# Residual kept by chunks, merged operands split in two portions, norms on two tiles, and early MLP weights split ahead of time in a transformer block on one core

## The chip, the cores and the metric

The kernel runs on one core of one Trainium2 chip. The metric is device time in microseconds (us) of one execution; the number for a kernel is the median of several timed runs. Engines: PE is the matrix engine, PEld its weight loads, DVE the vector engine, ACT the scalar engine, POOL is GpSimd, and SP is the engine whose queue issues nearly all DMAs of this kernel. Each engine takes its own instructions strictly in the order in which they were built, and waits at an instruction until what it needs is there.

## The reference, cut to what matters

One block on 1024 positions of 1024 channels behind 16 meta tokens (L = 1040), all in float32:

```
h      = rmsnorm(h_res, g_mix_pre)
u, c, b, v, gates = split(h @ w_in)
y_a    = fourier_mix(u) @ w_fourier            # real part of a 2-D DFT
y_b    = (b * dwconv3(c * v)) @ w_conv_out
merged = gates_0 * y_a + gates_1 * y_b
h_res  = h_res + rmsnorm(merged @ w_out, g_mix_post)
h2     = rmsnorm(h_res, g_ffn_pre)
a, v   = split(dwconv3(h2 @ w_up))             # 2 x 2816 columns
h_res  = h_res + rmsnorm((gelu(a) * v) @ w_down, g_ffn_post)
```

## The kernel before, in words

Activations lie transposed: a tile has 128 channels on the partitions and positions along the row, so 1024 channels are 8 tiles (`KT`). Every float32 matmul is made of three products of rounded operands of type fp32r (`mm3`, L163, L165, L167): an operand is *split* into a rounded part `hi`, a copy on ACT (L131, shown as CAST), and the rest `lo`, a subtraction on DVE (L132); the three products are hi·hi, lo·hi and hi·lo. The large products are made in seven pieces out of four quarters (`b11`, `t1`, `t2`, ...), whose sums and splits are kept in long-lived tiles of a pool (`room`, by tags such as `t1h`, `t3l`).

In order of time:

1. **Projection** (until about 310 us). A list of jobs, one pair of weight blocks each. Raw weights come by SP through a ring of three 512 KB buffers (`ring.raw`), are split, and are used from a ring of split pieces. Hooks in the jobs do work for later stages: `transformed(kt)` loads `wu` into a raw buffer (L609), PE multiplies it (L612, tile `wp`), ACT copies the product back into the same buffer, SP stores it (L617); `fold(kt)` loads, scales and folds the input on DVE and stores it.
2. **Fourier stage and merge** (to 424 us). The gated sum goes to DRAM as `merged_d`.
3. **Output projection** (424 to 523 us). Positions are cut into four chunks of 256 or 258 (`CHM`). `project(c)` makes, for each of 8 output tiles f, 8 times 3 matmuls on 258 columns, tile `mo`; the operands `mh`, `ml` are the split merged tiles of that chunk, the weights are resident. After each f, ACT squares `mo` and copies it, scaled, into `hA` (chunks 0, 1) or `hB` (chunks 2, 3). After some f a hook of other work is placed, at the level of priority of the newest matmul (`behind(x)` means: not ahead of x in the built order). The order inside an engine's queue is then fixed by the scheduler that builds the program. The hooks of chunk c are:
   - after f number 1, `norm_a(c-1)`: sum of squares (`ms_m` on PE), the reciprocal root `rr` (one ACT, three DVE instructions, L172 to L175), then per tile `hA = hA*rr`, plus the residual input `xr`, square on ACT, sum `sq_h` on DVE, and a store of the tile to DRAM as `hres_d` (needed again at the very end of the kernel);
   - after number 5, `load_merged(c+1)` (L929): three loads into raw buffers (`mr`), each followed by the splits of its three tiles into `mh` and `ml` (10 buffers each);
   - after number 6, `norm_b(c-1)` (L1003): `ms_h` on PE (L926), the root, then per tile a scaling (L1011) and the split into the MLP's operand `b11h`, `b11l`, `b21h`, `b21l` (chunks 0, 1), or a difference and the split into `t1`, `b22` (chunks 2, 3).
   In chunk 3 the hooks also load and split the first MLP weights (`plain.load`, `first_blocks`).
4. **Early MLP** (523 to 570 us). While the last two chunks are still normalised, PE works through products that need only the first half of the positions: `plain.first(...)` and `early(step, i)` for i from 1 to 5. Their weights go through the raw ring into rooms by `first_blocks`: 512 KB, two ACT casts and two DVE subtractions per block. Results that are kept for later are copied from the accumulator by ACT (`up_u`, L294; `up_1e`, L1104; `up_s`, L1060), and the accumulators are few, so PE waits for those copies.
5. **MLP** (to about 1000 us): 22 pairs of blocks, each followed by convolution, gelu and a product, with pieces stored in DRAM; then the **down projection** and the last norm, which loads `hres_d` again (`load_residual`) and stores the output.

What sets the order around the change: the hooks' places, the `behind` lines, three raw buffers, ten `m` buffers, four buffers of the tag `o` for `xr`, and the single SP queue for all DMAs.

Of the kernel before, what the change touches and what calls it, by code (L numbers as in the profile page):

```python
# [17 lines left out]
P = 128  # L18
# [25 lines left out]
CHM = [(0, 258), (258, 258), (513, 258), (771, 256)]  # L44
HALF = 512
# [45 lines left out]
def block_kernel(ctx, tc, xT, w_u, w_in, w_fa, w_fa2, w_fb, w_fb2, w_co, w_out, w_up, w_dn,  # L91
# [586 lines left out]
    W = 258  # L678
# [147 lines left out]

    def merged_parts(c, kt, src):
        n = src.shape[-1]
        parts = [
            op.tile([P, W], F32R, tag=f"m{i}", name=f"m{i}{c}_{kt}", bufs=10)[:, :n] for i in "hl"  # L830
        ]
        return parts, split(*parts, src)
# [96 lines left out]
    def load_merged(c):  # L929
        c0, n = CHM[c]  # L930
        v = valid(c)
        parts = []
# [7 lines left out]
        merged[c] = parts  # L940
# [32 lines left out]
    def norm_a(c):  # L973
        c0, n = CHM[c]
        v = valid(c)
        ms = next(z[c])
        rr = np_.tile([P, W], F32, tag="rr", name=f"rr{c}", bufs=2)[:, :n]
        got = rsqrt_of(f"r2_{c}", scratch, ms, n, rr)
        sq = squares(f"h{c}", n)
        next(sq)  # L980
        xr = []
        for f in range(0, KT, 2):
            t = eo.tile([P, 2 * W], F32, tag="o", name=f"xr{c}_{f}", bufs=4)
            t = t.rearrange("p (f n) -> p f n", f=2)
            SP.dma_start(t[:, :, :v], xT[:, f : f + 2, TM + c0 : TM + c0 + v])
            xr += [t[:, i, :v] for i in range(2)]
        for f in range(KT):
            h = h_at(c, f)
            scaled = mul(h, h, rr).ins
            add(h[:, :v], h[:, :v], xr[f])  # L990
            sq.send(h)
            SP.dma_start(hres_d[:, f, c0 : c0 + v], h[:, :v])
        z[c] = sq
        return got, scaled
# [8 lines left out]
    def norm_b(c):  # L1003
# [5 lines left out]
        for f in range(KT):  # L1009
            h = h_at(c, f)  # L1010
            V.scalar_tensor_tensor(out=h, in0=h, scalar=col("g_fpre", f), in1=rr, op0=ALU.mult, op1=ALU.mult)  # L1011
# [15 lines left out]
    def sums(c):  # L1027
        j, n = CHM[c][0] - 513, CHM[c][1]
        A, B = second(c)
        for f in range(4):  # L1030
            sub(A(f), B(f + 4), A(f))
            put(hx["t2"], f, A(f), j, n)
# [8 lines left out]

    class Plain:
# [5 lines left out]
        def load(self, row, name):  # L1048
            r = room(name, F32R, f"pw{row}")
            q = [r[:, k * 512 : (k + 1) * 512] for k in range(4)]  # L1050
            self.w[row] = early_pieces(f"{self.up.name}p{row}", srcs(self.up)[row], (q[:2], q[2:]))
# [120 lines left out]
    def first_blocks(*rooms_):  # L1172
        for n in rooms_:
            i = len(ep)
            into = (None, None)
            if n is not None:
                r = room(n, F32R, f"ep{i}")
                q = [r[:, k * 512 : (k + 1) * 512] for k in range(4)]
                into = (q[:2], q[2:])
            ep.append(early_pieces(firsts[i].name, srcs(firsts[i])[0], into))  # L1180
# [10 lines left out]
    project(0, {4: new_banks, 5: lambda: load_merged(1)})  # L1191
# [348 lines left out]
```

## Time and profile before

| what | us |
|---|---|
| median of 3 runs (lowest, highest) | 1206.96 (1206.75, 1207.26) |
| the profiled execution | 1208.31 |
| its span, first to last instruction | 1206.5 |
| PE busy, share of the span | 1177.1, 98% |
| DVE busy | 1000.9, 83% |
| ACT busy | 552.0, 46% |
| POOL busy | 8.4, 1% |

The profiled execution took 1.35 us more than the median, and 1.81 us of it lie outside the span. Times of day in this text ("at 468 us") are microseconds from the start of that span. In a row of instructions, the first number is the start, the second the busy time of the group, then come engine, line, operation, output<-inputs and shape; an idle time in brackets at the end is the wait just before the group and what ended it. Buffer numbers are left out in those names: `mh` may be any of `mh2_0` to `mh2_7`. In a table of stretches, the columns are the stretch, its length, busy us and number of instructions of PE, PEld, DVE, ACT and POOL, then the granted clock of PE as a share of full speed, the busy share of the DMA engines and the GB/s that they moved.

### The profile page before, as it was taken

The numbers are of one execution on the slowest core, as the hardware profiler recorded it, in microseconds if no ns is written. First come the engines' busy times: TensorE is split into PE (matmuls) and PEld (weight loads), VectorE is DVE, ScalarE is ACT, GpSimd is POOL, SyncE is SP. The second block draws the span as 40 slices with busy tenths as digits, with TensorE's granted clock in tenths as the row PEclk, the third lists the DMA queues.
The fourth block names the chain that finished last, engine by engine and source line by source line (L and its number), as shares of the span: only waits on it lengthen the run. The fifth ranks groups of instructions, "written<-read, shape, count | busy, mean of one in ns | idle before, by whom it ended". The sixth has DMA issues, their size and how long they took to land.

```text
span 1206.5 us, 22298 instructions
## 1 busy us (share of the span) xinstructions
PE 1177.1 (98%) x8790; PEld 1134.4 (94%) x8790; DVE 1000.9 (83%) x1756; ACT 552.0 (46%) x1008; POOL 8.4 (1%) x38
## 2 busy tenths in 40 slices
PE   8999999999999999998999999999999999999995
PEld 7999999999999999998999999999999998888884
DVE  8999976756578956989799999989988989856678
ACT  6743333223352345656544544444344444455562
POOL 0000000000020000000000000000000000000000
PEclk9999999999999999999999999999999999999998
DMA  6336655132876756575243334324323498354433
GB/s 250 123 111 217 194 177 176 53 132 90 276 232 223 256 169 106 141 101 153 98 143 106 121 122 149 123 97 131 97 71 96 139 331 315 101 167 126 135 119 140
DMA packets 79408, 184.25 MB, mean 153 GB/s; under 512 B 8146, under 2 KB 25778, under 8 KB 79304
## 3 DMA queue, kind: packets, MB, share of 16 engines
q1 hardware_dynamic: 79160, 182.71, 48.3%
q8 instruction: 69, 1.13, 0.4%
q14 instruction: 35, 0.29, 0.1%
q10 hardware_dynamic: 144, 0.12, 0.0%
HBM read 131.54 MB, written 51.26 MB: 152 GB/s over the span
## 4 chain that ended last, share of the span: by engine, by line
PE 81%; DVE 12%; DMA 4%; ACT 1%; issue 1%; SPq 0%; DVEq 0%; ACTq 0%
PE up_d L167 3%; PE up_c L165 3%; PE up_c L163 3%; PE up_d L163 3%; PE up_d L165 3%; PE up_c L167 3%; PE up_a L163 3%; PE up_a L167 3%; PE up_a L165 3%; PE dna L163 3%; PE dna L165 3%; PE dna L167 3%; PE dnb L165 2%; PE dnb L163 2%; PE dnb L167 2%; PE up_b L167 2%
## 5 line engine op out<-in xcount | busy, mean ns | idle before, releaser
L163 PE MATMUL mo<-mh,wo 128*128 128x258 f32 (+1 forms) x256 | 74.0, 289 | 0.0
L167 PE MATMUL mo<-mh,wo 128*128 128x258 f32 (+1 forms) x256 | 73.0, 285 | 0.0
L165 PE MATMUL mo<-ml,wo 128*128 128x258 f32 (+1 forms) x256 | 72.9, 285 | 0.0
L165 PEld LDWEIGHTS mo<-ml,wo 128*128 128x128 f32 x256 | 49.3, 193 | 0.2
L163 PEld LDWEIGHTS mo<-mh,wo 128*128 128x128 f32 x256 | 49.2, 192 | 0.2
L167 PEld LDWEIGHTS mo<-mh,wo 128*128 128x128 f32 x256 | 49.2, 192 | 0.0
L131 ACT CAST up_1h<-up_1t 128x512 fp32r<-128x512 f32 x11 | 6.8, 621 | 75.0 <-DVE up_1t L148 52.2
L1134 ACT ACTIVATE up_0o<-up_0o 128x512 f32<-128x512 f32 x44 | 27.8, 631 | 23.5 <-DVE up_0o L1132 23.3
L1130 ACT ACTIVATE up_1o<-up_1x,pr 128x512 f32<-128x512 f32 x33 | 26.9, 816 | 23.0 <-DVE up_1x L148 22.5
L167 PE MATMUL up_d<-b22h,up_5l 128*128 128x258 f32 (+1 forms) x168 | 34.2, 284 | 0.0
L165 PE MATMUL up_c<-t3l,up_3h 128*128 128x258 f32 (+1 forms) x168 | 34.1, 285 | 0.0
L167 PE MATMUL up_b<-t2h,up_2l 128*128 128x258 f32 (+1 forms) x168 | 34.0, 283 | 0.0
L163 PE MATMUL up_d<-b22h,up_5h 128*128 128x258 f32 (+1 forms) x168 | 34.0, 283 | 0.0
L165 PE MATMUL up_d<-b22l,up_5h 128*128 128x258 f32 (+1 forms) x168 | 33.9, 283 | 0.0
L165 PE MATMUL up_b<-t2l,up_2h 128*128 128x258 f32 (+1 forms) x168 | 33.9, 283 | 0.0
L163 PE MATMUL up_c<-t3h,up_3h 128*128 128x258 f32 (+1 forms) x168 | 33.8, 282 | 0.0
L163 PE MATMUL up_b<-t2h,up_2h 128*128 128x258 f32 (+1 forms) x168 | 33.8, 282 | 0.0
L163 PE MATMUL up_c<-t4h,up_6h 128*128 128x258 f32 (+1 forms) x168 | 33.8, 282 | 0.0
L163 PE MATMUL up_d<-t1h,up_1h 128*128 128x258 f32 (+1 forms) x168 | 33.7, 282 | 0.0
L167 PE MATMUL up_d<-t1h,up_1l 128*128 128x258 f32 (+1 forms) x168 | 33.7, 282 | 0.0
L165 PE MATMUL up_d<-t1l,up_1h 128*128 128x258 f32 (+1 forms) x168 | 33.6, 281 | 0.0
L167 PE MATMUL up_c<-t3h,up_3l 128*128 128x258 f32 (+1 forms) x168 | 33.6, 281 | 0.0
(1337 smaller groups left out, 4319.3 us busy)
## 6 DMA issues: line engine op xcount, KB each, us to landing
g<-gp_d SPq DMA_DIRECT2D x35, 512.0 KB, 4.2
up_1r<-in_w_up_dram SPq DMA_DIRECT2D x22, 512.0 KB, 3.6
gp_d<-up_0o SPq DMA_DIRECT2D x44, 256.0 KB, 2.0
up_0r<-in_w_up_dram SPq DMA_DIRECT2D x20, 512.0 KB, 4.1
s<-sig_d SPq DMA_DIRECT2D x16, 514.0 KB, 6.1
sig_d<-g_s SPq DMA_DIRECT2D x30, 257.0 KB, 3.4
u<-fold_d SPq DMA_DIRECT2D x8, 777.0 KB, 4.2
fold_d<-fold SPq DMA_DIRECT2D x8, 521.0 KB, 3.5
```

The costliest lines, as they stand in the source:

```text
L131: a = copy(hi, src)
L163: nc.tensor.matmul(o, wh, h, start=first, stop=False, **kw)
L165: nc.tensor.matmul(o, wh, l, start=False, stop=False, **kw)
L167: newest[:] = [nc.tensor.matmul(o, wl, h, start=False, stop=last, **kw).ins]
L1130: S.activation(t, ap[:, 1 : 1 + HALF], AF.Identity, bias=col("cb_ffn", b), scale=w(1))
L1134: S.activation(t, t, AF.Gelu_apprx_tanh)
```

## The change

**Residual by chunks.** The host passes the residual input a second time as `x_res`, laid out as [chunk, partition, tile, 258]; `hres_d` gets the same layout. A load of `xr` still brings two tiles, but as one run of 2064 bytes per partition in place of two of 1032. `norm_a` works on two tiles at once (multiply by `rr`, add `xr`), and stores two tiles with one DMA: four stores per chunk for eight. `load_residual` at the end makes two loads for each one, because a half of the positions spans two chunks.

**Norms on two tiles.** In `norm_b` and `sums` the scalings stay one tile each, but the differences and the splits (cast and subtraction) take two tiles each.

**Merged operands in two portions.** `load_merged(c+1)` moves from hook 5 to hook 0 (to 3 in chunk 0) and only issues the loads. The splits of tiles 0 to 2 (`MORE = 3`) are at hook 5. Those of tiles 3 to 7 are at hook 7, `last_parts`, behind the ACT casts of `b11` that `norm_b` just made. The `m` tiles get 11 buffers. The memset of the padding goes to GpSimd.

**Early MLP weights.** In projection jobs, at six hooks, `ahead(i)` loads one pair of weight blocks through the raw ring, splits it (two casts, two subtractions on 512 columns) and stores the four parts in DRAM (`split_d`) with four DMAs of 256 KB on GpSimd's queue. `plain.load` and `first_blocks` no longer load raw weights and split; they bring both parts, `hi` and `lo`, with two DMAs of 512 KB each on GpSimd's queue (`split_weights`). Only the last block (`first_blocks(None)`) goes on as before.

The number of PE instructions and their order do not change.

```
 def ahead(i):                                       # new, hooks (NE1 + i, 6), i = 0..5
     for n, parts in enumerate(ring.halves(f"ew{i}", w_up[EARLY_ROWS[i]])):
         for m, t in enumerate(parts):
             at = 512 * (2 * n + m)
             nc.gpsimd.dma_start(split_d[i, :, at : at + 512], t.bitcast(F32))

 def split_weights(i, name):                         # new, for plain.load and first_blocks
     r = room(name, F32R, f"ew{i}")[:, : 4 * 512]
...
     for k in range(0, 4, 2):
         at = slice(k * 512, (k + 2) * 512)
         nc.gpsimd.dma_start(r[:, at].bitcast(F32), split_d[i, :, at])

 def norm_a(c):
...
-            SP.dma_start(t[:, :, :v], xT[:, f : f + 2, TM + c0 : TM + c0 + v])
+            SP.dma_start(t, x_res[c, :, f : f + 2])
...
-        for f in range(KT):
-            h = h_at(c, f)
-            scaled = mul(h, h, rr).ins
-            add(h[:, :v], h[:, :v], xr[f])
-            sq.send(h)
-            SP.dma_start(hres_d[:, f, c0 : c0 + v], h[:, :v])
+        for f in range(0, KT, 2):
+            h = h_two(c, f)
+            scaled = mul(h, h, rr[:, None, :].to_broadcast([P, 2, n])).ins
+            add(h, h, xr[f // 2])
+            for i in range(2):
+                sq.send(h_at(c, f + i))
+            SP.dma_start(hres_d[c, :, f : f + 2, :n], h)

 def load_merged(c):
...
-                V.memset(t[:, :, v:], 0.0)
-            parts += [merged_parts(c, kt, t[:, kt - k])[0] for kt in range(k, e)]
+                nc.gpsimd.memset(t[:, :, v:], 0.0)
+            merged_r[c, k] = t
+def split_merged(c, ks):
+    for kt in ks:
+        merged[c].append(merged_parts(c, kt, merged_r[c, kt // 3 * 3][:, kt % 3])[0])
+def last_parts(c):
+    with behind(*cast):                              # cast: the b11 casts of norm_b
+        split_merged(c, range(MORE, KT))
...
-            1: lambda: norm_a(c - 1), 5: lambda: load_merged(c + 1), 6: lambda: (mean_b(c - 1), norm_b(c - 1)),
+            0: lambda: load_merged(c + 1), 1: lambda: norm_a(c - 1), 5: lambda: split_merged(c + 1, range(MORE)),
+            6: lambda: (mean_b(c - 1), norm_b(c - 1)), 7: lambda: last_parts(c + 1),
```

What the change moves is seen in the built order. First DVE at the boundary of chunk 1 and chunk 2, from the second root (`r3_0_t`, `rrb0`) of chunk 0 on. Before (`hA0`, `hA1` are the two halves of the tiles of chunk 0, `ml2_3` is the `lo` of the merged tile 3 of chunk 2):

```order
L173 SCALAR_TENSOR_TENSOR r3_0_t_5778<-r3_0_y_5777 128x258
L132 TENSOR_TENSOR ml2_2_5718<-mr2_0_5707,mh2_2_5717 128x258
L132 TENSOR_TENSOR ml2_3_5724<-mr2_3_5721,mh2_3_5723 128x258
L132 TENSOR_TENSOR ml2_4_5728<-mr2_3_5721,mh2_4_5727 128x258
L132 TENSOR_TENSOR ml2_5_5732<-mr2_3_5721,mh2_5_5731 128x258
L132 TENSOR_TENSOR ml2_6_5738<-mr2_6_5735,mh2_6_5737 128x258
L132 TENSOR_TENSOR ml2_7_5742<-mr2_6_5735,mh2_7_5741 128x258
L174 SCALAR_TENSOR_TENSOR r3_0_t_5778<-ms_h0_5774,r3_0_t_5778 128x258
```

The same place of DVE's queue in the changed kernel:

```order
L176 SCALAR_TENSOR_TENSOR r3_0_t_5831<-r3_0_y_5830 128x258
L177 SCALAR_TENSOR_TENSOR r3_0_t_5831<-ms_h0_5827,r3_0_t_5831 128x258
L178 SCALAR_TENSOR_TENSOR rrb0_5829<-r3_0_t_5831,r3_0_y_5830 128x258
L1040 SCALAR_TENSOR_TENSOR hA0_5245<-hA0_5245,pr_68,rrb0_5829 128x258 x4
L135 TENSOR_TENSOR b11l_5252<-hA0_5245,b11h_5251 128x2x257
L1040 SCALAR_TENSOR_TENSOR hA1_5246<-hA1_5246,pr_68,rrb0_5829 128x258
L135 TENSOR_TENSOR b11l_5252<-hA0_5245,b11h_5251 128x2x257
L1040 SCALAR_TENSOR_TENSOR hA1_5246<-hA1_5246,pr_68,rrb0_5829 128x258 x3
L151 TENSOR_TENSOR sq_m1_0_5580<-sq_m1_0_5580,sq_m1_7_5877 128x258
L135 TENSOR_TENSOR b21l_5254<-hA1_5246,b21h_5253 128x2x257 x2
L135 TENSOR_TENSOR ml2_3_5882<-mr2_3_5585,mh2_3_5881 128x258
L135 TENSOR_TENSOR ml2_4_5886<-mr2_3_5585,mh2_4_5885 128x258
```

Tiles 3 to 7 of the next chunk's merged operand stood behind one instruction of the root and now stand behind the whole of `norm_b(0)`. On PE, the matmul that reads `ml2_3` is the second one of tile 3, the eleventh of chunk 2 (nine matmuls on tiles 0 to 2 come first). At the boundary of chunks 2 and 3 the order has the same form.

SP's queue in the projection, around the second hook of weights that are split ahead (`wu` of `transformed`, `V0r` raw weights of a later job, `sig_d` and `fold_d` stores). Before:

```order
L617 DMA fold_d_58<-wu1_2153 128x512
L395 DMA sig_d_57<-g0_3_s22_2103 128x514
L204 DMA V0r0_2271<-in_w_in_dram 128x1024
L395 DMA sig_d_57<-g0_3_s11_2188 128x514
L204 DMA V0r1_2273<-in_w_in_dram 128x1024
L395 DMA sig_d_57<-g0_3_s12_2219 128x514
L609 DMA wu2_2402<-in_w_u_dram 128x512
```

And in the changed kernel:

```order
L624 DMA fold_d_58<-wu1_2168 128x512
L402 DMA sig_d_57<-g0_3_s22_2118 128x514
L207 DMA ew1r_2286<-in_w_up_dram 128x1024
L402 DMA sig_d_57<-g0_3_s11_2203 128x514
L207 DMA V0r0_2300<-in_w_in_dram 128x1024
L402 DMA sig_d_57<-g0_3_s12_2234 128x514
L207 DMA V0r1_2302<-in_w_in_dram 128x1024
L402 DMA sig_d_57<-g0_3_s21_2278 128x514
L641 DMA fold_d_58<-fold6_3545 128x1042
L616 DMA wu2_2431<-in_w_u_dram 128x512
```

The ring has three raw buffers and goes round: before, `wu2` takes the buffer that `wu1` had; now, with one load more per job, it takes the one that `ew1r` had. On ACT in the early MLP, the changed kernel has these rows (`up4_1e_0h` and `up1_0_0h` are split from the raw loads `up4_1er` and `up1_0r0`; `up1_1_a` is an accumulator of PE):

```order
L297 COPY up1_1_u_6819<-up1_1_a_6794 128x514
L175 ACTIVATE r3_3_y_6977<-ms_h3_6824,eps_t_72 128x256
L134 CAST up4_1e_0h_6988<-up4_1er_6986 128x512
L134 CAST up4_1e_1h_6992<-up4_1er_6986 128x512
L134 CAST up1_0_0h_7055<-up1_0r0_7051 128x512
L1148 COPY up1_1e_6854<-up1_1_a_6794 128x514
```

In the kernel before, the copy `up1_1e` stands ahead of the casts from `up4_1er` and `up1_0r0`, and behind two pairs of casts of `ep3`.

More of the change, by code (lines that the diff above doesn't have):

```diff
@@ L365, in put, with put2 @@
         split(hi[:, kt, c0 : c0 + n], lo[:, kt, c0 : c0 + n], src, eng=eng)
+    def put2(piece, kt, src, c0=0, n=NH):
+        hi, lo = piece
+        return split(hi[:, kt : kt + 2, c0 : c0 + n], lo[:, kt : kt + 2, c0 : c0 + n], src)
     proj_s = ExitStack()
@@ L654, in next_fold, with ahead @@
         folded.append((xs, (hi[:, FW:w], lo[:, FW:w])))
+    EARLY_ROWS = [0, NF // 2, *(NF + n // 2 for n in EARLY[:-1])]
+    def ahead(i):
+        for n, parts in enumerate(ring.halves(f"ew{i}", w_up[EARLY_ROWS[i]])):
+            for m, t in enumerate(parts):
+                at = 512 * (2 * n + m)
+                nc.gpsimd.dma_start(split_d[i, :, at : at + 512], t.bitcast(F32))
     hooks = {(NE1 + kt, 3): lambda kt=kt: transformed(kt) for kt in range(KT)}
+    for i in range(len(EARLY_ROWS)):
+        hooks[NE1 + i, 6] = lambda i=i: ahead(i)
     for kt in range(KT):
@@ L829, in merged_parts @@
         parts = [
-            op.tile([P, W], F32R, tag=f"m{i}", name=f"m{i}{c}_{kt}", bufs=10)[:, :n] for i in "hl"
+            op.tile([P, W], F32R, tag=f"m{i}", name=f"m{i}{c}_{kt}", bufs=KT + MORE)[:, :n] for i in "hl"
         ]
@@ L931, in load_merged @@
         v = valid(c)
-        parts = []
+        merged[c] = []
         for k in range(0, KT, 3):
@@ L1029, in sums @@
         A, B = second(c)
-        for f in range(4):
+        for f in range(0, 4, 2):
             sub(A(f), B(f + 4), A(f))
-            put(hx["t2"], f, A(f), j, n)
+            put2(hx["t2"], f, A(f), j, n)
             sub(B(f), B(f + 4), B(f))
@@ L1040, in block_kernel, with split_weights @@
     place = {}
+    def split_weights(i, name):
+        r = room(name, F32R, f"ew{i}")[:, : 4 * 512]
+        q = [r[:, k * 512 : (k + 1) * 512] for k in range(4)]
+        for k in range(0, 4, 2):
+            at = slice(k * 512, (k + 2) * 512)
+            nc.gpsimd.dma_start(r[:, at].bitcast(F32), split_d[i, :, at])
+        return q[:2], q[2:]
     class Plain:
@@ L1048, in load @@
         def load(self, row, name):
-            r = room(name, F32R, f"pw{row}")
-            q = [r[:, k * 512 : (k + 1) * 512] for k in range(4)]
-            self.w[row] = early_pieces(f"{self.up.name}p{row}", srcs(self.up)[row], (q[:2], q[2:]))
+            self.w[row] = split_weights(row, name)
         def first(self, row, part):
@@ L1174, in first_blocks @@
             i = len(ep)
-            into = (None, None)
             if n is not None:
[L1177 to L1180, printed above, removed]
+                ep.append(split_weights(i + 1, n))
+            else:
+                ep.append(early_pieces(firsts[i].name, srcs(firsts[i])[0]))
     def second_half():
@@ L1376, in load_residual @@
         hr[:] = [tiles_in(at + i, f"hr{half}{i}") for i in range(2)]
+        h0 = NM - TM + half * HALF
         for i in range(2):
-            SP.dma_start(hr[i], hres_d[:, 4 * i : 4 * i + 4, 2 + half * HALF : 2 + (half + 1) * HALF])
+            at = 0
+            for c in (2 * half, 2 * half + 1):
+                a = h0 + at - CHM[c][0]
+                n = min(CHM[c][1] - a, HALF - at)
+                SP.dma_start(hr[i][:, :, at : at + n], hres_d[c, :, 4 * i : 4 * i + 4, a : a + n])
+                at += n
+            assert at == HALF
     def finish(half, rr, work, o=0, n=HALF):
@@ L1480 @@
     xT = np.ascontiguousarray(h.T.reshape(KT, P, L).transpose(1, 0, 2))
+    x_res = np.zeros((len(CHM), P, KT, W), np.float32)
+    for c, (c0, n) in enumerate(CHM):
+        part = xT[:, :, TM + c0 : TM + c0 + n]
+        x_res[c, :, :, : part.shape[2]] = part
     wf = a["w_fourier"][0].reshape(G, P, D)
```

41 lines of the change are left out of this document (29 added, 12 removed).

## The prediction

> **What bounds the kernel now.** I read the page first, then the stretches of 10 us around the edited code, the list of PE's waits, and the rows of each engine where PE waits. The page and the stretches:
>
> ```profile
> PE 1177.1 (98%) x8790; PEld 1134.4 (94%) x8790; DVE 1000.9 (83%) x1756; ACT 552.0 (46%) x1008; POOL 8.4 (1%) x38
> ...
> 100.00:310.00 210.00, 210.00 (x1760) 210.00 (x1759) 155.70 (x249) 71.68 (x128) 0.00 (x0) 1.00 0.46 147
> 480.00:490.00 10.00, 10.00 (x86) 10.00 (x85) 10.00 (x29) 5.72 (x16) 0.00 (x0) 1.00 0.14 30
> 490.00:500.00 10.00, 7.47 (x48) 7.21 (x47) 8.54 (x26) 7.27 (x22) 0.00 (x0) 0.83 0.81 191
> 530.00:540.00 10.00, 8.12 (x68) 7.91 (x67) 6.64 (x19) 3.37 (x10) 0.00 (x0) 1.00 0.22 57
> 540.00:550.00 10.00, 6.89 (x53) 6.49 (x54) 9.68 (x30) 5.50 (x13) 0.00 (x0) 0.99 0.77 183
> 550.00:560.00 10.00, 9.32 (x65) 9.12 (x64) 8.53 (x20) 5.32 (x11) 0.00 (x0) 0.84 0.57 196
> 560.00:570.00 10.00, 10.00 (x86) 10.00 (x84) 9.65 (x29) 6.58 (x16) 0.00 (x0) 1.00 0.29 95
> ```
>
> PE is the bound, busy 98%. Its instructions are not touched, so a gain can only be a wait of PE that goes, a loss one that comes. A stretch in which nothing is late holds 86 matmuls, so one takes 10/86 = 0.116 us; what a stretch lacks of 86 is lost time, waits and slow clock together. The stretch from 490 lacks 38, or 4.4 us. Those from 530, 540 and 550 lack 18, 33 and 21, together 72, or 8.4 us. The waits and the rows behind them:
>
> ```profile
> PE up_a L163 <- ACT up_u L294: 3.0, 2, 2.6
> PE ms_h L926 <- DVE sq_h L148: 2.5, 1, 2.5
> PE up_z L163 <- ACT up_s L1060: 2.4, 1, 2.4
> ...
> PE up_a L163 <- ACT up_1e L1104: 0.7, 1, 0.7
> ```
>
> ```profile
> 478.94 0.71 ACT L131 CAST mh<-mr 128x256 fp32r<-128x256 f32 x2 [6.58 <-DMA mr<-merged_d]
> 480.00 1.44 DVE L132 TENSOR_TENSOR b11l<-hA,b11h 128x257 fp32r<-128x257 f32 x4 [5.38 <-ACT b11h L131]
> 494.70 0.74 PE L926 MATMUL ms_h<-sq_h,ones 128*128 128x258 f32 x2 [2.53 <-DVE sq_h L148]
> 533.29 0.49 DVE L1011 SCALAR_TENSOR_TENSOR hB<-hB,pr,rrb 128x258 f32<-128x258 f32 x1 [3.29 <-DMA hres_d<-hB]
> 537.48 6.34 SPq L992 DMA_DIRECT2D hres_d<-hB  x8
> ```
>
> The stall at 494.70 has a clear history. ACT stands 6.58 us in front of the casts of the next chunk's merged tiles, whose load was issued in the same hook. Behind those casts are the casts of `b11`, so DVE waits 5.38 us, then `norm_a` of chunk 1 is late, and PE finds no `sq_h`. In the early MLP, DVE waits 3.29 us until a store of `hres_d` has landed, because `norm_b` overwrites that tile, and eight stores in SP's queue keep the weight loads behind them.
>
> **What goes in the output projection.** The merged loads are issued six output tiles before their first cast, so the 6.58 us on ACT go, and with them the stall at 494.70. Of its 4.4 us, 2.5 are the wait and 1.9 the lower clock after it (0.83 in that stretch). I take −4.4. It could be less only if another wait took that place; the next one in line is below.
>
> **What comes there.** At the boundary of chunks 1 and 2, DVE now runs all of `norm_b` before the `lo` of merged tile 3. The rows of before give each duration:
>
> ```profile
> 468.08 0.59 PE L926 MATMUL ms_h<-sq_h,ones 128*128 128x258 f32 x2
> 468.33 0.47 PE L163 MATMUL mo<-mh,wo 128*128 128x258 f32 x1
> ```
>
> ```profile
> 468.92 0.48 ACT L172 ACTIVATE r_y<-ms_h,eps_t 128x258 f32<-128x258 f32 x1
> 469.28 2.02 ACT L131 CAST mh<-mr 128x258 fp32r<-128x258 f32 x6
> 560.87 0.62 ACT L131 CAST up_0h<-up_0r 128x512 fp32r<-128x512 f32 x1 [1.34 <-DMA up_0r<-in_w_up_dram]
> ```
>
> ```profile
> 455.97 0.43 DVE L173 SCALAR_TENSOR_TENSOR r_t<-r_y 128x258 f32<-128x258 f32 x1 [1.73 <-ACT r_y L172]
> 457.36 0.77 DVE L154 TENSOR_TENSOR hA<-hA,rr 128x258 f32<-128x258 f32 x2
> 469.43 0.43 DVE L173 SCALAR_TENSOR_TENSOR r_t<-r_y 128x258 f32<-128x258 f32 x1 [0.30 <-ACT r_y L172]
> 469.78 2.11 DVE L132 TENSOR_TENSOR ml<-mr,mh 128x258 fp32r<-128x258 f32 x6
> 472.94 1.68 DVE L1011 SCALAR_TENSOR_TENSOR hA<-hA,pr,rrb 128x258 f32<-128x258 f32 x4
> 573.91 2.50 DVE L132 TENSOR_TENSOR t3l<-hB,t3h 128x514 fp32r<-128x514 f32 x4
> ```
>
> PE makes `ms_h` at 468.08, and nothing of the root can be earlier. DVE begins the root at 469.43, and from its first instruction to the first use of the result it takes 457.36 − 455.97 = 1.39 us, so `norm_b` begins at 470.82. Then come 8 scalings of 1.68/4 = 0.42 (3.36), 4 subtractions on two tiles of 2.50/4 = 0.62 (2.50), one sum of squares and `ml2_3` itself, each priced by the row of the `ml` group at 2.11/6 = 0.35 (0.70). `ml2_3` is there at 470.82 + 6.56 = 477.4. PE is faster: it begins the last output tile of chunk 1 at 468.33, has 24 matmuls there and 9 on tiles 0 to 2 of the next chunk, then one with `mh2_3`, 34 × 0.116 = 3.9, and wants `ml2_3` at 472.3. It waits 5.1 us. The wait has two pieces, since `mh2_3` stands on ACT behind the second cast of `b11`: 470.82 + 4 × 0.42 + 0.62, and its own 2.02/6 = 0.34 or so, gives 473.5 at the earliest, so about 1.3 us first and 3.8 after one matmul. After that each tile costs DVE 0.35 and PE three matmuls, 0.35, so nothing is won back. Before, the six `ml` stood ahead of the rest of the root, and there was no wait. The boundary of chunks 2 and 3 has the same order and so the same price: 2 × 5.1 = +10.2.
>
> To this comes the clock. A wait of 2.53 us was followed by 0.83 at a price of 1.9; one of 2.4 in the stretch from 530 left it at 1.00. A piece of 3.8 us lies beyond both, so I take 1.9 for each boundary, +3.8, with 0 as the other end. [...]
>
> The norms on two tiles save DVE and ACT some instructions, but both wait for PE or are waited for only at the places above: nothing. The added memset on GpSimd stands before no one's work but the splits of tiles that come much later: nothing, and at most 0.43 us, the longest of its ordinary rows shown below, if the cover is gone.
>
> **The early MLP.** What is lost now is 8.4 us. The change takes away the eight stores (four are left, so SP is through in about half of the 6.34 us), and twelve casts with their subtractions. The waits for `up_s` (2.4) and the longer one for `up_u` (2.6) should go: I read both as copies in ACT's queue behind casts that waited for DVE, and DVE was late by those 3.29 us and by the norm on single tiles. What is late next: the copy `up1_1e` of the accumulator, for which PE waits 0.7 now, stands behind three casts that need the raw loads `up4_1er` and `up1_0r0`.
>
> ```profile
> 554.21 0.59 ACT L1104 COPY up_1e<-up_a 128x514 f32<-128x514 f32 x1 [3.00 <-PE up_a L167]
> ```
>
> That copy ran at 554.21. The cast of `up1_0r0` ran at 560.87 when its load was there, so if that load is as late as now, the copy is late by 560.87 + 0.62 − 554.21 = 7.3. If the load comes when the queue ahead of it is empty, it is 0. Two raw loads ahead of it in the ring are gone, so I take a little under half, 3.0, and a slow clock for 1.9. With the waits that stay (of `up_u` 3.0 − 2.6 = 0.4, of `up_1e` 0.7) that is 6.0 after for 8.4 before: −2.4. The ends are 1.1 after, −7.3, and 1.1 + 7.3 + 1.9 = 10.3 after, +1.9.
>
> **The projection.** Six jobs get a load of 512 KB, two casts, two subtractions and four stores.
>
> ```profile
> 187.15 0.33 SPq L609 DMA_DIRECT2D wu<-in_w_u_dram  x1
> 196.99 1.05 PE L612 MATMUL wp<-dc,wu 128*128 128x128 f32 x8
> ...
> wu<-in_w_u_dram SPq DMA_DIRECT2D x8, 256.0 KB, 2.8
> gp_d<-up_0o SPq DMA_DIRECT2D x44, 256.0 KB, 2.0
> ```
>
> DVE is busy 155.7 of 210 us and ACT 71.7, so 12 subtractions and 12 casts of about 0.62 each (7.4 on either) fit. What can be late is `wu`: its buffer is now the one that `ew` just left, and SP holds everything behind it. It now lands 196.99 − 187.15 − 2.8 = 7.0 us before PE wants it. Below, the price is 0; above, five loads (the first has none ahead) that use up those 7.0 us and land 1.0 late each are 5. I take +1.0, since the slack of 7.0 is more than the load's own time. The six blocks move 6 MB in later loads where 3 MB were, at DMA shares of 0.22 to 0.81 in their stretches; that is in the bounds above.
>
> **The end.** `load_residual` has 4 DMAs more, early in a stage in which SP has room: nothing, at most the 0.33 us of an issue each.
>
> **Sum.** −4.4 + 10.2 + 3.8 − 2.4 + 1.0 = +8.2 us. Against the profiled execution, 1208.31 (span 1206.5 and 1.81 around it), that is 1216.5; that execution lies 1.35 above the median of the runs, so for the median 1206.96 + 8.2 = 1215.2.
>
> **The rivals.**
>
> *The clock stays full.* Then the boundaries cost 10.2 and the early MLP loses 4.1: −4.4 + 10.2 − 4.3 + 1.0 = +2.5, or 1209.5. For it speaks the 1.00 after a wait of 2.4; against it 0.83 after 2.53 and 0.84 in the stretch from 550. Chance 0.15.
>
> *The early MLP is freed (the other side).* If the raw loads land before the copy at 554.21, that is, some 7 us sooner than now, PE loses only 1.1 there: −7.3. With a full clock at the boundaries and a free projection the sum is −4.4 + 10.2 − 7.3 = −1.5, or 1205.5: faster. Each boundary of less than 4.6 in place of 5.1 (PE a little later, DVE's instructions a little shorter) takes it below 1204.5. For it speaks that SP's queue is emptier; against it that the rows fix DVE's chain at the boundary, and that a clock was lost after 2.53 us. It decides by a boundary's price with its clock: at 5.8 gain and loss are even. Chance 0.15.
>
> *GpSimd's queue is slow beside DVE.* Rows of GpSimd and DVE:
>
> ```profile
> 343.08 0.43 POOL L774 CAST stackedh<-pqh 105x4 fp32r<-105x4 f32 x3
> 343.44 2.77 POOL L774 CAST stackedl<-pql 105x4 fp32r<-105x4 f32 x3
> ```
>
> ```profile
> 340.43 3.56 DVE L132 TENSOR_TENSOR pql<-pq,pqh 105x512 fp32r<-105x512 f32 x5 [1.62 <-ACT pqh L131]
> 343.90 0.42 DVE L148 TENSOR_TENSOR wfa<-wfa 128x256 f32<-128x256 f32 x1
> ```
>
> The same three casts take 0.43 while DVE reads accumulators, and 2.77 when it goes over to operations that read two ordinary tiles: 2.3 us more. If each store on GpSimd's queue is held up so, it takes 2.0 + 2.3 = 4.3, four of them 17.2 us of a job, which is 168 matmuls of 210/1760 = 0.119, or 20.0. The split pieces stay taken, 2.8 us are left, and load and two subtractions (2.8 + 1.2) come 1.2 late in six jobs: +7.2 on top of the sum, 1222.4. Against it: no row shows a DMA of that queue beside DVE. Chance 0.15. [...]
>
> **How the numbers follow.** The forecast's case has what is left, 0.55: 1215.2, and with its own bounds (clock at one boundary only, early MLP 2 us either way, projection 0 to 5) 1211 to 1220. The range reaches down through the first rival, 1209.5, with the early MLP better by 2: 1207.5; and up to the third with the upper end of the early MLP: 1224. Left out are the second rival and the upper end of the third. About 0.2% (2.4 us) is what a measurement of this kernel tells from no change. Faster by more than that is somewhat over half of the second rival, 0.09; within it the rest of that and a little of the first, 0.07; slower 0.84.
>
> **What would show it.** In the changed profile, PE should wait in the first matmuls of chunks 2 and 3 for `mh` and then `ml` (L135), some 5 us at each, with a stretch at a clock near 0.83; ACT's wait for `mr` and PE's wait for `sq_h` near 494 should be gone; PE should lose about 6 us between 530 and 570, most of it for `up_1e`; `wp` should wait little. If PE runs through both boundaries, the main term is wrong. If `wp` or `ew` appears among PE's longest waits, the projection term is.

## The result, and the profile after

The changed kernel takes 1216.75 us (median of 5 runs, 1215.88 to 1221.06) for 1206.96 (median of 5, 1203.90 to 1211.45): a ratio of 1.008, 95% interval 1.0061 to 1.0099. The forecast was 1215.2. The profiled execution took 1219.75, 3.0 above the median, with a span of 1218.0 for 1206.5: 11.5 us more, in which the clock of PE was 0.985 on average; the runs near the median had 0.989 and 0.990. So this trace shows somewhat more lost clock than a run at the median.

To see where the 11.5 us lie, I cut the span at the first matmul of certain tiles, which is the same work in every kernel here: `wp` (154.97 before, 154.95 after), `pq` (311.59 and 317.42), `mo` (424.37 and 429.81), `up_z` (523.16 and 538.15), and the first MLP matmul on `t3` (593.28 and 604.15).

| stage, us | before | after | difference |
|---|---|---|---|
| projection, `wp` to `pq` | 156.6 | 162.5 | +5.9 |
| Fourier and merge, `pq` to `mo` | 112.8 | 112.4 | −0.4 |
| output projection, `mo` to `up_z` | 98.8 | 108.3 | +9.5 |
| early MLP, `up_z` to `t3` | 70.1 | 66.0 | −4.1 |
| rest | 613.2 | 613.9 | +0.7 |

The stretches of the changed kernel that answer to those of before (columns as there):

```profile
100.00:310.00 210.00, 204.81 (x1711) 204.27 (x1710) 159.26 (x255) 77.54 (x139) 13.10 (x24) 1.00 0.56 185
...
470.00:480.00 10.00, 8.41 (x67) 7.95 (x65) 7.73 (x19) 6.69 (x20) 0.00 (x0) 1.00 0.43 122
480.00:490.00 10.00, 7.35 (x41) 7.29 (x42) 4.95 (x13) 3.41 (x10) 0.21 (x2) 0.66 0.24 65
490.00:500.00 10.00, 10.00 (x85) 10.00 (x84) 9.09 (x19) 4.32 (x12) 0.00 (x0) 1.00 0.52 109
500.00:510.00 10.00, 8.89 (x73) 8.62 (x71) 6.56 (x16) 5.58 (x17) 0.00 (x0) 1.00 0.39 104
510.00:520.00 10.00, 6.91 (x37) 6.72 (x38) 4.75 (x12) 3.08 (x9) 1.09 (x2) 0.66 0.14 36
...
560.00:570.00 10.00, 8.09 (x55) 7.88 (x54) 7.48 (x16) 3.29 (x7) 1.06 (x2) 0.83 0.88 327
```

Each boundary of two chunks lacks matmuls in two stretches of 86 each: 19 + 45 = 64, and 13 + 49 = 62, that is 7.4 and 7.2 us at 0.116 each. The projection lacks 1760 − 1711 = 49. PE's waits, the longest first:

```profile
PE mo L168 <- DVE ml L135: 5.9, 2, 3.0
PE wp L619 <- DMA wu<-in_w_u_dram: 5.2, 3, 2.1
PE mo L166 <- ACT mh L134: 2.5, 2, 1.3
...
PE up_a L166 <- ACT up_1e L1148: 1.9, 1, 1.9
```

The wait for `sq_h` (2.5 before) and the one for `up_s` (2.4) are gone, `up_u` has 0.2 left. In their place stand `ml` and `mh` at the boundaries, and `wu` in the projection. At the first boundary, the rows of PE and of DVE:

```profile
479.29 0.38 PE L166 MATMUL mo<-mh,wo 128*128 128x258 f32 x1 [1.26 <-ACT mh L134]
482.65 0.58 PE L168 MATMUL mo<-ml,wo 128*128 128x258 f32 x1 [2.97 <-DVE ml L135]
```

```profile
474.84 0.43 DVE L176 SCALAR_TENSOR_TENSOR r_t<-r_y 128x258 f32<-128x258 f32 x1 [0.30 <-ACT r_y L175]
...
476.23 1.68 DVE L1040 SCALAR_TENSOR_TENSOR hA<-hA,pr,rrb 128x258 f32<-128x258 f32 x4
...
482.18 2.77 DVE L135 TENSOR_TENSOR ml<-mr,mh 128x258 fp32r<-128x258 f32 x8
```

From the root's first instruction to the first scaling DVE took 476.23 − 474.84 = 1.39, and from there to `ml` 5.95 (forecast 6.56 with the `ml` itself, so 6.21). PE waits in the two pieces that were worked out.

### The profile page after: what moved, and what is told of

Read it like the earlier page. It is cut to its first block, busy times and chain, and to the rows that moved or that the text cites. A ratio compares the mean times of both kernels' runs of the same rounds, so it can differ in the third digit from the quotient of the medians.

```text
span 1218.0 us, 22314 instructions
## 1 busy us (share of the span) xinstructions
PE 1181.7 (97%) x8790; PEld 1137.7 (93%) x8790; DVE 999.5 (82%) x1685; ACT 550.5 (45%) x988; POOL 28.2 (2%) x77
## 4 chain that ended last, share of the span: by engine, by line
PE 83%; DVE 10%; DMA 4%; ACT 1%; issue 1%; DVEq 0%; SPq 0%; ACTq 0%
PE up_a L166 3%; PE up_d L170 3%; PE up_c L168 3%; PE up_d L166 3%; PE up_c L166 3%; PE up_d L168 3%; PE up_c L170 3%; PE up_a L170 3%; PE up_a L168 3%; PE dna L170 3%; PE dna L166 3%; PE dna L168 3%; PE mo L168 2%; PE dnb L170 2%; PE dnb L166 2%; PE dnb L168 2%
## 5 line engine op out<-in xcount | busy, mean ns | idle before, releaser
L166 PE MATMUL mo<-mh,wo 128*128 128x258 f32 (+1 forms) x256 | 75.6, 295 | 2.5 <-ACT mh L134 2.5
L170 PE MATMUL mo<-mh,wo 128*128 128x258 f32 (+1 forms) x256 | 74.2, 290 | 0.0
L166 PEld LDWEIGHTS mo<-mh,wo 128*128 128x128 f32 x256 | 50.5, 197 | 3.1 <-ACT mh L134 2.9
L170 PEld LDWEIGHTS mo<-mh,wo 128*128 128x128 f32 x256 | 50.8, 198 | 0.0
L151 DVE TENSOR_TENSOR sq_m<-sq_m,sq_m 128x258 f32<-128x258 f32 (+1 forms) x28 | 12.0, 427 | 30.2 <-ACT sq_m L941 30.2
```

Source lines behind the costliest of these rows:

```text
L151: return eng.tensor_tensor(out=out, in0=a, in1=b, op=ALU.add).ins
L166: nc.tensor.matmul(o, wh, h, start=first, stop=False, **kw)
L170: newest[:] = [nc.tensor.matmul(o, wl, h, start=False, stop=last, **kw).ins]
```

## The experiments

Twelve kernels, in three groups (e1, e2, e5, e7; e3, e4, e6, e8; e9 to e12), each group on one chip with its own runs of the kernel before. Between the chips that kernel's median went from 1204.2 to 1209.2, so a ratio says less across groups than its interval does: the versions below with a span of 1196.9 and 1197.1 had ratios of 0.9973 and 0.9910. Where a part of the time is assigned, it is by the stages of the traces. A trace is one execution, from 2.6 us below the median of its kernel (e2) to 4.7 above (e9). Three of the stages, cut as above:

| kernel | ratio (95%) | projection | output projection | early MLP | span |
|---|---|---|---|---|---|
| before | 1 | 156.6 | 98.8 | 70.1 | 1206.5 |
| changed | 1.0080 (1.0061 to 1.0099) | 162.5 | 108.3 | 66.0 | 1218.0 |
| e1 splits ahead | 1.0006 (0.9991 to 1.0021) | 161.8 | 94.5 | 66.2 | 1202.4 |
| e2 splits between | 1.0034 (1.0020 to 1.0048) | 161.3 | 96.7 | 65.2 | 1203.8 |
| e3 weights as before | 1.0021 (1.0006 to 1.0037) | 156.6 | 108.1 | 63.2 | 1208.5 |
| e4 weights alone | 1.0097 (1.0068 to 1.0127) | 166.6 | 98.9 | 75.8 | 1222.3 |
| e5 portions alone | 1.0073 (1.0059 to 1.0088) | 156.6 | 108.8 | 65.6 | 1212.9 |
| e6 two tiles and layout | 0.9923 (0.9901 to 0.9946) | 156.6 | 94.5 | 64.0 | 1197.0 |
| e7 wu in its own buffer | 0.9973 (0.9958 to 0.9989) | 156.5 | 94.5 | 65.0 | 1196.9 |
| e8 splits ahead, no weights | 0.9912 (0.9888 to 0.9936) | 156.6 | 94.5 | 64.4 | 1197.4 |
| e9 two-tile instructions | 1.0028 (1.0012 to 1.0043) | 156.6 | 101.8 | 73.5 | 1216.0 |
| e10 layout alone | 0.9925 (0.9906 to 0.9945) | 156.7 | 94.5 | 65.3 | 1201.2 |
| e11 copy first | 0.9910 (0.9890 to 0.9930) | 158.2 | 94.5 | 63.2 | 1197.1 |
| e12 early loads alone | 0.9953 (0.9930 to 0.9976) | 156.6 | 94.5 | 68.1 | 1199.8 |

Of the stages left out, the rest took 613.0 to 614.8, and the Fourier stage 110.6 to 112.8 but for e9 and e10, 115.5 and 115.6. PE waits there 1.5 and 1.9 for a cast of `u`, with half the clock for 3.41 us behind it. No edit of these two kernels touches that stage, and why they wait is not known.

**e1, all splits ahead of the norm.**

```
...
-            5: lambda: split_merged(c + 1, range(MORE)),
-            6: lambda: (mean_b(c - 1), norm_b(c - 1)), 7: lambda: last_parts(c + 1),
+            5: lambda: split_merged(c + 1, range(KT)),
+            6: lambda: (mean_b(c - 1), norm_b(c - 1)),
...
```

> The changed kernel, but all eight merged tiles of the next chunk are split from hook 5 on, so that tiles 3 to 7 stand ahead of norm_b on DVE and ACT as before the change. Theory (the loss at the two chunk boundaries is the order of DVE, 64 and 62 matmuls short in the changed profile, 14.6 us): PE waits for no ml and no mh there, and the time falls from 1216.75 to about 1202. Rival A (the waits come from the loads of the merged tiles or from fewer m buffers): the waits stay, 1214 to 1217. Rival B (the old stall near 494 comes back, since ACT has the casts of the next chunk early again): PE waits again for sq_h, some 4 us of the 14.6 are lost, about 1206.

The output projection fell from 108.3 to 94.5, 13.8 us for 14.6 expected; PE waits neither for `ml` nor for `mh`, and the old wait for `sq_h` did not come back. Both rivals fall. The whole time fell less than expected: from a ratio of 1.0080 to 1.0006 is 8.9 us. The spans of the two traces are 15.6 apart, but the changed kernel was timed apart from this group and profiled 3.0 above its median; the rest of that gap is not explained.

**e2, splits between the halves of the norm.**

```
...
+    def norm_and_parts(c):
+        mean_b(c - 1)
+        norm_b(c - 1, range(4))
+        last_parts(c + 1)                # without behind(*cast)
+        norm_b(c - 1, range(4, KT))
...
```

> The changed kernel, but tiles 3 to 7 are split between the two halves of norm_b: on DVE ml2_3 to ml2_5 come between the instructions of the root, ml2_6 behind four scalings, ml2_7 behind two b11l subtractions as well. Theory (order of DVE): by the durations of the prediction only ml2_7 is late, at 474.8 for 473.7 on the clock of before, so PE waits about 1 us at each boundary, and after so short a wait the clock stays at 1.00: about 1204. Rival (any wait at the boundary costs the clock, 3 us each): about 1210.

The rows of that kernel, PE's wait and the stretch that holds it:

```profile
479.35 0.39 PE L168 MATMUL mo<-ml,wo 128*128 128x258 f32 x1 [0.89 <-DVE ml L135]
```

```profile
470.00:480.00 10.00, 9.11 (x74) 8.84 (x74) 8.01 (x20) 7.37 (x22) 0.20 (x2) 1.00 0.41 105
```

A longest wait of 0.89 for about 1 forecast, and the clock stays at 1.00 in that stretch: the order of DVE sets the wait, and short ones (three, 1.5 in all) did not cost the clock in this execution. It lies 2.6 below its kernel's median, though: by the medians e2 is 3.2 us slower than e1 on the same chip (1208.19 and 1204.97), by the spans 1.4. So it is not shown that such waits never cost the clock. The 8 us by which the rival set e2 behind e1 are not there.

**e5, the portions alone, on the kernel before.** The new hooks, `split_merged` and `last_parts`, with single tiles, old layout and old weights.

> The kernel before with the two portions of merged operands alone (loads at hook 0, tiles 3 to 7 behind the b11 casts); residual, norms on single tiles and early weights as before. Theory (the order at the boundary is the cost, the loads at hook 0 the gain): -4.4 near 494 and +14.6 at the two boundaries on 1206.96, about 1217; single tiles make norm_b on DVE longer (8 subtractions of 0.35 for 4 of 0.62, 0.3 more), so PE's waits there are 5 us or a little over. Rival (the boundary only costs together with the two-tile norms): about 1203 to 1207.

The output projection took 108.8 for 98.8, with the same waits (6.0 for `ml`, 2.7 for `mh`). So the boundary's price belongs to the portions, not to their meeting with the two-tile norms. The early MLP fell to 65.6 although nothing in it was changed. The same loads without these stalls give 68.1 (e12), so 2.5 of the 4.5 us hang on the stalls. That DVE and ACT get ahead while PE stands is the likely way, and was not shown.

**e7, `wu` in a buffer of its own (with the splits of e1).**

```
-        r = ring.raw(f"wu{kt}")
+        r = pre.tile([P, 1024], F32, tag="wu", name=f"wu{kt}", bufs=1)
```

> The kernel with all merged splits ahead of norm_b, and wu in a buffer of its own in place of one of the raw ring, so that its load does not wait for the split of ew; SP issues it right behind the store of the wu before. Theory A (wp is late because SP reaches the load of wu only when ew has left its buffer, 4.6 us ahead of PE in place of 12): PE waits no more for wu, the 5.2 us of waits for wu in the changed profile go, 4 to 6 us below the kernel with the splits alone. Theory B (wp is late because the four stores on GpSimd's queue fill the DMA engines, share 1.0 for 8 us, and every load beside them lands late): PE then waits for other weights instead, and no more than 2 us are won.

First the changed kernel (issue of `wu` and its matmuls, then the stretches between), then e7:

```profile
194.80 0.33 SPq L616 DMA_DIRECT2D wu<-in_w_u_dram  x1
201.51 1.13 PE L619 MATMUL wp<-dc,wu 128*128 128x128 f32 x8 [2.12 <-DMA wu<-in_w_u_dram]
```

```profile
194.00:196.00 2.00, 2.00 (x18) 2.00 (x18) 0.69 (x1) 0.04 (x1) 1.08 (x2) 1.00 1.03 413
196.00:198.00 2.00, 2.00 (x19) 2.00 (x18) 1.39 (x2) 0.36 (x1) 0.00 (x0) 1.00 1.03 377
198.00:200.00 2.00, 1.38 (x12) 1.17 (x10) 0.65 (x2) 0.26 (x1) 0.00 (x0) 1.00 0.98 294
```

```profile
182.47 0.33 SPq L616 DMA_DIRECT2D wu<-in_w_u_dram  x1
197.49 1.06 PE L619 MATMUL wp<-dc,wu 128*128 128x128 f32 x8
```

In the changed kernel `wu` is issued 6.7 us before its matmul, and the DMA engines are full (share about 1.0) from 194 to 200, with four stores of 256 KB on GpSimd's queue, issued from 191.57 to 195.06, and SP's own transfers. In e7 it is issued 15.0 us before, the projection is back at 156.5, and the kernel is 4.3 us faster than e1 (medians of 1200.69 and 1204.97). Theory A holds: the buffer delays the issue, and with it free the waits go. The late landing is theory B's part: 6.7 us for a load that lands after 2.8 in the kernel before. Either alone would have fitted, as an estimate from these rows: PE was ready 201.51 − 2.12 − 194.80 = 4.6 us after the late issue, more than 2.8, and 6.7 is less than the 9.8 from issue to matmul in the kernel before. The late landing was not taken away by itself.

**e3, early weights as before (the rest as changed).** No `ahead`, and `plain.load` and `first_blocks` as in the kernel before.

> The changed kernel with the early MLP weights loaded and split in place as before the change; portions, residual and two-tile norms stay. Theory 1 (in the changed kernel the early MLP is faster because PE's two stalls of some 5 us at the boundaries give DVE and ACT time to catch up; so it was with the portions alone, where the stage from the first up_z to the first t3 took 65.6 us for 70.1): the projection is free of waits for wu (-5.1 to -5.8 against the changed kernel), the boundaries stay, the early MLP stays near 66: ratio to the kernel before about 1.004. Theory 2 (the twelve casts and subtractions that left ACT and DVE freed it): the early MLP goes back to about 70: ratio about 1.008.

The projection is free again, and the early MLP is not slower than in the changed kernel but faster, 63.2 for 66.0. Theory 2 falls: taking casts and subtractions off ACT and DVE freed nothing that was missed. The weights by way of DRAM cost there too: PE waits 0.7 for `up_1e` in e3 and 1.9 in the changed kernel, with the clock of 0.83 behind it.

**e4, early weights alone, on the kernel before.** `ahead`, `split_d` and `split_weights` only.

> The kernel before with the early MLP weights split in the projection and kept in DRAM alone. Both theories: waits for wu in the projection, +5 us. Theory 1 of the early MLP: that stage stays near 70, as the norms and the stores of hres_d are as before: 1.004. Theory 2: it falls to about 66: 1.001. The stall for sq_h near 494 stays in both.

Worse than both expected: the projection took 166.6, 10 us more, and the early MLP 75.8. In the projection PE waits 3.5 for `wu` and 2.9 for a sum of DVE, and the clock is at half for 6.83 us from 245.57, which is another 3.4. Rows of the early MLP:

```profile
539.96 0.55 PE L164 MATMUL up_a<-b11h,ew 128*128 128x258 f32 x1 [2.96 <-DMA ew<-split_d]
...
569.17 0.79 PE L164 MATMUL up_a<-b11h,ew 128*128 128x258 f32 x2 [5.19 <-ACT up_1e L1121]
```

PE waits for a block itself, and 5.19 us for the copy `up_1e`.

**e6, residual layout and two-tile norms alone, on the kernel before.**

> The kernel before with the residual by chunks and the norms on two tiles alone; merged operands and early weights as before. What it tells: how much of the early MLP and of the stall near 494 comes from the stores of hres_d (four for eight) and from the shorter norms. If these are the cause of the early MLP's waits, that stage falls from 70.1 to 66 or 67 and the ratio is about 0.997; if not, it stays at 1.000. The projection stays at 156.6 from the first wp to the first pq in either case.

The output projection fell to 94.5 and the early MLP to 64.0: this part of the change alone is a gain of 0.8%. The forecast had nothing for it in the output projection, and −2.4 us in the early MLP for it and the weights together.

**e8, splits ahead and weights as before.** The edits of e1 and e3 together.

> The changed kernel with all merged splits ahead of norm_b and with the early weights loaded and split in place as before. No stalls at the boundaries, none for wu. Theory 1 (slack from the boundary stalls freed the early MLP): without them the early MLP goes back to near 70, so -4.3 for the chunks and no more: ratio about 0.9965. Theory 2 (weights freed it): the same number. Theory 3 (the two-tile norms and fewer stores freed it): 66, ratio about 0.993, and better than the version with wu in a buffer of its own.

Theory 3: 64.4 in the early MLP and a ratio of 0.9912. With the new layout and two-tile norms the stage is fast without any stall at the boundaries.

**e9 and e10, the two halves of e6.** e9 takes only the instructions on two tiles, e10 only the layout:

```
 e9:  for f in range(0, KT, 2): mul and add on h_two(c, f); then per tile
          SP.dma_start(hres_d[:, f + i, c0 : c0 + v], h[:, i, :v])
 e10: for f in range(KT): mul and add on h_at(c, f); at odd f
          SP.dma_start(hres_d[c, :, f - 1 : f + 1, :n], h_two(c, f - 1))
```

> The kernel before with two-tile instructions in norm_a, norm_b and sums alone; xr and hres_d keep their old layout, loads of 1032 bytes a row and one store per tile. Two tiles and layout together took the output projection from 98.8 to 94.5 and the early MLP from 70.1 to 64.0. Theory I (the shorter norms did it): this kernel shows nearly all of it, ratio about 0.992. Theory D (the DMAs did it: longer rows, half the stores, so that the load of mr lands 3.5 after its issue in place of 8.7): the stage of the output projection stays near 98.8 and the early MLP gains little, ratio 0.998 to 1.000.

> The kernel before with the new layouts of x_res and hres_d, their loads of 2064 bytes a row and one store per two tiles alone; every instruction of the norms on one tile as before. Theory I: 1.000, with the wait for sq_h near 494. Theory D: the wait near 494 goes (output projection 94.5) and most of the early MLP's gain is here, ratio about 0.993.

Theory D, and clearly: 0.9925 with the layout, 1.0028 with the instructions. e9 is even worse than theory D expected (101.8 and 73.5 for 98.8 and 70.1), in an execution 4.7 above its median. Three kernels at the place where the merged tiles of chunk 3 are loaded. The issue on SP or the cast that waits, and the fullest stretch there; first the kernel before:

```profile
470.23 2.47 SPq L936 DMA_DIRECT2D mr<-merged_d  x3
```

```profile
460.00:470.00 10.00, 10.00 (x84) 9.94 (x83) 8.10 (x23) 6.76 (x20) 0.00 (x0) 1.00 1.08 168
```

Then e10:

```profile
474.15 2.05 SPq L957 DMA_DIRECT2D mr<-merged_d  x3
477.68 0.72 ACT L134 CAST mh<-mr 128x256 fp32r<-128x256 f32 x2 [1.40 <-DMA mr<-merged_d]
```

```profile
460.00:470.00 10.00, 10.00 (x86) 10.00 (x85) 9.58 (x27) 3.98 (x11) 0.00 (x0) 1.00 0.61 151
```

And e9:

```profile
484.55 0.71 ACT L131 CAST mh<-mr 128x256 fp32r<-128x256 f32 x2 [9.11 <-DMA mr<-merged_d]
```

```profile
470.00:480.00 10.00, 10.00 (x83) 9.94 (x83) 6.05 (x19) 4.34 (x13) 0.00 (x0) 1.00 1.26 103
```

In the old layout the residual's loads and stores keep the DMA engines full (share 1.08 and 1.26) at 168 and 103 GB/s, and the merged load, issued last, lands 478.94 − 470.23 = 8.7 us later. In the new one the share is 0.61 at 151 GB/s, and the load lands 3.5 us after its issue. In e9 the wait grows to 9.11; that a shorter norm issues the same transfers closer together is the likely reason, not shown. Which part of the gain is the rows of 2064 bytes and which the four stores for eight was not tried apart.

**e12, the merged loads at hook 0 alone, on the kernel before.** e5 with the splits of e1.

> The kernel before with the merged loads issued at hook 0 alone; all splits from hook 5 on, ahead of norm_b, with 11 m buffers; single tiles, old layouts, old weights. The prediction's reason for -4.4 (the load that ACT waits for 6.58 us is issued late): the wait for sq_h near 494 goes, output projection 94.5, ratio about 0.9965. Rival (only the shorter norms or the fewer stores can take that wait away): it stays, 98.8, ratio 1.000. The early MLP stays near 70 in both.

94.5 and 0.9953: the reason that the prediction gave for −4.4 holds. (The early MLP, expected near 70, took 68.1.) But e10 takes the same wait away with the load at its old place. Either is enough, and together they give nothing more.

**e11, the copy ahead of the casts (on e7).**

```
-    with behind(*done):
+    with behind(*done, firsts[3].copied):      # the copy up1_1e
         first_blocks(None)
...                                                # the same ahead of the first job
```

> The version with all splits ahead and wu in its own buffer, and in the early MLP the casts of the last block and of the first job are held behind the copy up1_1e. Theory (PE's wait of 2.1 for up_1e is ACT standing in casts whose raw load has not landed): the wait falls to about 0.7, 1.4 us less there, early MLP 63.5 for 65.0. Rival (the late weights of GpSimd's queue are next in line): PE waits for ew or for the last block instead, and nothing is won.

The changed kernel at that place, ACT, and then e11, PE:

```profile
562.19 0.62 ACT L134 CAST up_1e_0h<-up_1er 128x512 fp32r<-128x512 f32 x1 [2.33 <-DMA up_1er<-in_w_up_dram]
...
563.97 0.58 ACT L1148 COPY up_1e<-up_a 128x514 f32<-128x514 f32 x1
```

```profile
545.78 0.51 PE L166 MATMUL up_a<-b11h,ew 128*128 128x258 f32 x2 [0.68 <-ACT up_1e L1148]
```

The wait fell from the 2.13 of e7 to 0.68 and the early MLP from 65.0 to 63.2, and nothing else took its place: the rival falls. (The projection took 158.2 for 156.5, with a wait of 1.4 for a sum of DVE at `wp`, which this edit does not touch.) With this repair the weights by way of DRAM are no longer a loss in that stage, but no gain over e8 either (0.9910 and 0.9912, on two chips).

## Why the prediction was right, and where it was not

- **The boundaries, +14.0 (10.2 of waits, 3.8 of clock): right in cause, and measured 64 + 62 matmuls, 14.6.** The order of DVE was the cause, as e1, e2 and e5 show. That the sum came so close is partly luck, since its two terms were off in opposite ways: waits of 8.4 for 10.2, clock of 6.2 for 3.8. The waits were 1.26 + 2.97 = 4.2 each for 5.1: DVE's chain was 0.3 shorter, and PE came to tile 3 later, 478.03 − 473.49 = 4.5 us after the start of its `ms_h` for 4.1. The clock took more, 7.4 − 4.2 = 3.2 and 7.2 − 4.2 = 3.0, for 1.9 each. That this was no freak of one execution is seen in e3 and e5, whose output projections took 108.1 and 108.8.
- **The stall at 494, −4.4: right in size and in its reason (e12).** For the norms on two tiles the prediction put "nothing", and e9 shows no gain by them. The new layout of the residual got no price in this stage; that was wrong for the layout by itself, which takes the same 4.3 us away (e10). The sum came out all the same, because the two remedies take away one and the same stall. The forecast counted stores only as SP's issue time, and row lengths not at all; as time of the DMA engines they were to be seen in the share of 1.08 at 168 GB/s in the stretch from 460.
- **The early MLP, −2.4: measured −4.1, and for another reason.** The layout gives 4.8 of it alone (65.3 in e10), shorter norms with it 6.1 (64.0 in e6). The forecast credited the twelve casts and subtractions as well; in truth the weights cost 66.0 − 63.2 = 2.8 there (changed kernel against e3), and 0.6 to 1.8 without the stalls at the boundaries (e7 and e1 against e8). The next wait was named rightly: the copy `up1_1e` behind casts of raw loads, 1.9 for 3.0, with a clock of 0.83 behind it.
- **The projection, +1.0 with an end of 5: measured +5.9, just past that end.** The place and the buffer were right (e7). The step that failed is the slack: 7.0 us were set against the load's 2.8, as if it would land alone. It is issued later and lands beside four stores and SP's own transfers, 6.7 us after its issue.
- **The end, 0:** 227.4 before and 228.0 after from the first down-projection matmul (979.14 and 990.02) to the end of the span. Nothing that can be told from noise.
- **The sum** is right, 1215.2 for 1216.75, since the boundaries bear it, but that it is within 1.6 is luck as well. Behind it, an error of −1.7 in the early MLP and one of +4.9 in the projection partly cancel. By the spans the loss is 11.5 us for the 8.2 forecast; by the medians it is 9.8, since the profiled execution of the changed kernel lies 3.0 above its median and that of the kernel before 1.35.
- **The rivals.** The clock did not stay full (0.66 at both boundaries). The early MLP was freed in part, 4.1 for the 7.3 of that rival, and the boundaries cost 7.3 with their clock, over the 5.8 at which gain and loss were even. GpSimd's queue was not slow beside DVE: two stores issued while DVE ran an instruction on two ordinary tiles took 0.54 each on GpSimd, as nearly all others did (0.54 to 0.68). The four stores of that round landed 3.3 to 4.5 us after their issue, with DVE busy 8.24 of the 9 us from 236 and a DMA share of 0.65; those of the round from 191 took 5.9 to 7.0, with DVE busy 4.06 of 10 us and a share of 0.90. So these stores take longer than the 2.0 of SP's row, but in these two rounds it goes with the load on the DMA engines and not with DVE. The rows of the two stores, and of DVE beside them:

```profile
238.77 0.54 POOL L669 DMA_DIRECT2D split_d<-ew_1h  x1 [1.34 <-ACT ew_1h L134]
239.30 0.54 POOL L669 DMA_DIRECT2D split_d<-ew_0l  x1
```

```profile
238.32 1.28 DVE L601 SCALAR_TENSOR_TENSOR t<-c,pr,t 128x1028 f32<-128x1028 f32 x1
```

## What to carry to other kernels

Where two pieces of work meet on one in-order engine, count in the built order what stands ahead of the operand that the bound engine needs first; that count, with durations from the trace, gave the waits of the largest term here, 8.4 us, as 10.2. Before crediting an edit with freeing an engine, look whether anyone waited for that engine's time or for its place in a queue; the weights split ahead freed time that nobody missed and cost transfers that somebody did. And a change of three parts is judged part by part: the residual layout alone was worth 0.75% (e10). With the two-tile norms it is 0.9923 (e6), with the early loads besides and without the order at the boundary and the weights 0.9912 (e8); these three cannot be told apart by their intervals.

## What the runs showed of the hardware that was not expected

In these traces the clock after a wait of PE did not follow from the length of the wait alone. Two kernels with the same wait at the same matmul, e1 and then e7:

```profile
549.05 0.51 PE L166 MATMUL up_a<-b11h,ew 128*128 128x258 f32 x2 [2.14 <-ACT up_1e L1148]
```

```profile
540.00:550.00 10.00, 7.61 (x60) 7.00 (x58) 7.51 (x16) 4.42 (x8) 1.07 (x2) 1.00 0.86 278
550.00:560.00 10.00, 10.00 (x73) 10.00 (x72) 8.90 (x18) 3.82 (x8) 0.00 (x0) 0.83 0.50 187
```

```profile
545.27 0.51 PE L166 MATMUL up_a<-b11h,ew 128*128 128x258 f32 x2 [2.13 <-ACT up_1e L1148]
```

```profile
540.00:550.00 10.00, 7.87 (x63) 7.66 (x64) 7.78 (x17) 4.10 (x9) 1.07 (x2) 1.00 0.90 325
550.00:560.00 10.00, 10.00 (x85) 10.00 (x85) 9.93 (x17) 6.97 (x14) 0.00 (x0) 1.00 0.21 80
```

After 2.14 us the clock was 0.83 in the next stretch, after 2.13 it was 1.00. Of 172 matmuls in the two stretches e1 lacks 39, or 4.5 us, and e7 24, or 2.8. The difference is 1.7 us.

The drops of the clock in the traces have a pattern that fits the difference. Between 30 and 1150 us each of them, 19 in 14 traces, is to half the clock and lasts 3.41 us or twice that, so it costs up to 1.7 or 3.4 us: in e1 from 550.38, in the kernel before from 495.25 and 549.86, in the changed kernel from 480.83 and 511.55 (6.83 each) and from 566.16. Within a trace these starts lie whole multiples of 3.41 apart: 511.55 − 480.83 = 9 × 3.413, and 566.16 − 511.55 = 16 × 3.413. Cut along that grid, the wait of e1 lies inside one piece, and the piece after it has half the clock; the wait of e7 is shared by two pieces, and no drop follows (e7 has no drop near, and its grid is continued from the one at 26.06):

```profile
546.97:550.38 3.41, 1.33 (x11) 1.33 (x12) 3.11 (x7) 1.89 (x4) 1.07 (x2) 1.00 0.71 194
550.38:553.79 3.41, 3.41 (x19) 3.41 (x18) 3.22 (x8) 0.23 (x1) 0.00 (x0) 0.50 0.93 370
```

```profile
541.47:544.88 3.41, 1.67 (x14) 1.47 (x13) 1.59 (x4) 1.90 (x4) 1.07 (x2) 1.00 0.80 316
544.88:548.30 3.42, 3.03 (x25) 3.03 (x26) 3.42 (x8) 0.34 (x1) 0.00 (x0) 1.00 0.88 256
```

PE is idle for 3.41 − 1.33 = 2.08 us of the first piece of e1, and for 1.74 and 0.39 of the two of e7. Each of the 19 drops follows a piece with 1.84 us or more of idle PE; of the pieces at full clock with that much, one is not followed by a drop (1.87, in the projection of e1). The wait of 2.4 in the kernel before, at a full clock, is shared by two pieces too (1.50 and 0.88). So in these traces a wait of some 2 us cost 1.7 or nothing, by where it fell on a grid that lies differently in each trace; the two waits at a boundary, 4.2 us within 4.6 in the changed kernel, were followed by 6.83 us of half the clock at all six boundaries of that kernel, e3 and e5. No experiment moved a wait along the grid, so that its place there decides is a reading of these drops and was not shown by a run of its own.
